# Token mixers of the second block: value products issued two blocks behind the scores, recurrence and convolution issued in pieces

## Chip, cores and metric

The kernel is one program on one core of a Trainium2 chip. The metric is the device time of one execution in microseconds. "Before" and "after" are the kernel without and with the change.

## What is computed

The reference is two transformer-like blocks over 1024 tokens of width 1024, all in float32. The change touches only the token mixers of the second block. With `xn` the normalised input, they are:

```python
proj = xn @ w_in[l]
u, g_lru, q, k, v, z = jnp.split(proj, splits, axis=-1)
uc = centred_depthwise_conv(u, conv_w[l], conv_b[l])
h_fwd = rg_lru(uc, lru_lambda[l, 0], ..., False)
h_bwd = rg_lru(uc, lru_lambda[l, 1], ..., True)
y_a = (h_fwd + h_bwd) * jax.nn.gelu(g_lru)
y_b = banded_alibi_sink_attention(q, k, v, attn_sink[l])
gates = jax.nn.sigmoid(z + b_gate[l]).reshape(bsz, s, N_BRANCH, D_MODEL)
merged = gates[:, :, 0] * y_a + gates[:, :, 1] * y_b
```

In `rg_lru`, two block-diagonal products of `uc` give r and i by a sigmoid, `log_a = -8 * r * softplus(-lam)`, `a = exp(log_a)`, `beta = sqrt(1 - a*a)`, and h is the scan h[t] = a[t] * h[t-1] + beta * i * uc, forwards or backwards in time. The attention has 16 query heads and 4 key/value heads; each block of 128 queries sees its own and the two neighbouring blocks of 128 keys, with a linear distance bias and a sink term in the softmax.

## The kernel before, in words

Every float32 operand is held as two parts, high and low, and a product is three matrix products (high by high, high by low, low by high; `gemm`, L163 to L165), over 128x512 outputs. A weight comes by DMA into `raw`; ScalarE writes its high part (L150) and GpSimd its low part (L151). `split` (L192, L193) does the same for other tensors.

`mixers` runs over j = 0..7; one such stretch is called a period here. Period j does the attention of two heads (`attention(j)`), the three projections of the gates of j (`gates`: g, and two of z), and for j+1 the projection u with its convolution (`lru_front`), the projection q (`att_pair`) and the recurrence's gate products (`lru_gates`). Each projection is two half products of 24 matrix products (`chunk(q)`, 512 tokens each). The recurrence behind the gate products (`lru_rest`) is elementwise: `decay` (ScalarE Exp and Tanh, VectorE L1482), `rate` (ScalarE Square, VectorE L1489 and L1490), `root` (ScalarE Sqrt, L1493, which needs another function table), `scan` (VectorE product L1497 and scans L1499 and L1502, GpSimd sum L1500). Its five pieces are issued one behind each half product of `gates` and, for j = 0, ahead of the half products.

The attention is a generator; `tick` advances it by one step, in the middle and at the end of each half product. Its steps alternate. One issues the scores of query block n+1 (`att_scores`, S below: products L1595 and L1596, the reducing VectorE instruction L1597, the softmax) and the value product of block n-1 (`att_values`, V: L1630, evacuated by ScalarE L1633 and VectorE L1635). The other issues the transposes of block n (`att_turned`, T: L1617, and the split into `pt`, L192 and L193). At j = 2, 4 and 6 the keys and values of the next head group are loaded (`att_group`) and split into `kq` and `vhl`. `merged` (L1685) joins the two branches.

PSUM has eight banks: `mm` three (projections), `ax` two (recurrence gates), `sc` two (scores and transposes), `po` one (value products). The `slot` pool has ten [128 x 1024] buffers, `kq` six, `pt` two. Each engine runs its instructions in one fixed order, which follows the order of issue; an instruction waits for its operands and for the release of its buffer.

## Time and profile before

| | before |
|---|---|
| device time, median of 3 | 3420.71 us (3416.87 to 3430.2) |
| profiled execution: time, span | 3423.95 us, span 3422.2 us |
| mean granted TensorE clock | 0.981 of full |
| TensorE (PE) busy | 3260.1 us, 95% of the span |
| VectorE (DVE), GpSimd (POOL), ScalarE (ACT) busy | 2126.6, 1539.2, 1363.1 us |

The mixers of the second block take the stretch from 1947 to 2650 us. Times below are from the start of the span. Idle time of an engine counts only where the engine that sets the end waits for it. The granted clock has two levels, 2.4 GHz (1.00) and 1.2 GHz (0.50).

### The profile page before, as it was taken

The page shows a single profiled execution, that of the slowest core. Times are in us where ns is not written, and L with a number is a line of the kernel's source. Part 1 is how long each engine was busy: PE and PEld are TensorE (multiplying, and loading weights), DVE is VectorE, ACT ScalarE, POOL GpSimd, SP SyncE. Part 2 cuts the span into 40 slices and gives each one's busy share as a digit, 9 for nine tenths or more (in the row PEclk, how much of TensorE's full clock was granted, in tenths as well). Part 3 has the DMA queues.
Part 4 walks back from the last instruction along what each step waited for, and adds up shares of the span by engine and source line. Part 5 has one row for each costly group of instructions (what it writes and reads, how often), then busy time and mean ns, then how long its engine had stood idle before and what let it go on. Part 6 is the DMA issues. An engine that isn't in the chain of part 4 may idle for free. (4 is left out here: it accounts for less than half of the span.)

```text
span 3422.2 us, 43238 instructions
## 1 busy us (share of the span) xinstructions
PE 3260.1 (95%) x15868; PEld 2695.3 (79%) x15868; DVE 2126.6 (62%) x3438; ACT 1363.1 (40%) x2396; POOL 1539.2 (45%) x991
## 2 busy tenths in 40 slices
PE   7999999999999999999989989999999999999998
PEld 4778888888888878888767867777777778888767
DVE  7554234333667386565798487777776585554786
ACT  4552122211122442222434486666665333233433
POOL 3222233221312775454655433444444775554764
PEclk9999999999999999999999999999999999999999
DMA  6121121244236522221342411111114422222342
GB/s 257 62 105 59 50 68 65 75 157 133 77 119 218 171 89 84 74 96 60 122 164 84 131 33 55 45 54 45 55 48 139 161 99 98 81 81 94 98 132 79
DMA packets 153012, 335.11 MB, mean 98 GB/s; under 512 B 20864, under 2 KB 29184, under 8 KB 152800
## 3 DMA queue, kind: packets, MB, share of 16 engines
q1 hardware_dynamic: 140640, 311.36, 27.5%
q10 hardware_dynamic: 12160, 20.98, 1.7%
q8 instruction: 126, 2.06, 0.3%
q14 instruction: 86, 0.70, 0.1%
HBM read 263.07 MB, written 69.21 MB: 97 GB/s over the span
## 5 line engine op out<-in xcount | busy, mean ns | idle before, releaser
L151 POOL TENSOR_TENSOR wl<-raw,wh 128x1024 fp32r<-128x1024 f32 (+1 forms) x188 | 426.1, 2271 | 742.7 <-ACT wh L150 666.1
L163 PE MATMUL mm<-hl,wh 128*128 128x512 f32 (+1 forms) x1584 | 636.8, 402 | 1.6 <-ACT t L1547 1.4
L165 PE MATMUL mm<-hl,wl 128*128 128x512 f32 (+1 forms) x1584 | 625.4, 395 | 2.8 <-POOL wl L151 2.8
L164 PE MATMUL mm<-hl,wh 128*128 128x512 f32 (+1 forms) x1584 | 624.2, 394 | 0.0
L193 POOL TENSOR_TENSOR wl<-half,wh 128x512 fp32r<-128x512 f32 x308 | 432.1, 1426 | 345.6 <-ACT wh L192 340.3
L150 ACT CAST wh<-raw 128x1024 fp32r<-128x1024 f32 (+3 forms) x189 | 177.3, 940 | 491.6 <-PE mm L164 215.7
L165 PEld LDWEIGHTS mm<-hl,wl 128*128 128x128 f32 (+1 forms) x1584 | 300.9, 190 | 68.0 <-POOL wl L151 3.6
L163 PEld LDWEIGHTS mm<-hl,wh 128*128 128x128 f32 (+1 forms) x1584 | 301.6, 190 | 59.5 <-ACT t L1547 1.8
L164 PEld LDWEIGHTS mm<-hl,wh 128*128 128x128 f32 (+1 forms) x1584 | 301.3, 190 | 58.1 <-issue 0.5
L192 ACT CAST wh<-half 128x512 fp32r<-128x512 f32 x308 | 178.5, 619 | 390.4 <-PE ax L1052 197.2
L1030 DVE TENSOR_TENSOR half<-half 128x512 f32<-128x512 f32 x176 | 204.4, 1200 | 3.0
L1606 POOL TENSOR_SCALAR p<-p,ast 128x384 f32<-128x384 f32 (+1 forms) x64 | 84.1, 1314 | 263.5 <-DVE ast L1604 172.5
L175 PE MATMUL mm<-wh,hl 128*128 128x256 f32 x576 | 166.1, 289 | 3.4 <-ACT wh L150 3.4
L177 PE MATMUL mm<-wl,hl 128*128 128x256 f32 x576 | 164.5, 286 | 1.9 <-POOL wl L151 1.9
L176 PE MATMUL mm<-wh,hl 128*128 128x256 f32 x576 | 164.5, 286 | 0.8 <-DVE hl L193 0.6
L1052 PE MATMUL mm<-hl,wh 128*128 128x512 f32 x360 | 140.6, 391 | 3.3 <-POOL hl L193 3.3
L1051 PE MATMUL mm<-hl,wh 128*128 128x512 f32 x360 | 140.3, 390 | 0.7 <-ACT hl L192 0.7
L1053 PE MATMUL mm<-hl,wl 128*128 128x512 f32 x360 | 140.3, 390 | 0.0
L1051 PE MATMUL ax<-hl,wh 128*128 128x512 f32 x344 | 134.2, 390 | 2.0 <-ACT hl L192 1.3
L1053 PE MATMUL ax<-hl,wl 128*128 128x512 f32 x344 | 134.1, 390 | 0.1
L1052 PE MATMUL ax<-hl,wh 128*128 128x512 f32 x344 | 133.9, 389 | 0.0
L193 POOL TENSOR_TENSOR wl<-raw,wh 128x384 fp32r<-128x384 f32 x96 | 113.1, 1198 | 39.4 <-ACT wh L192 38.8
(419 smaller groups left out, 7996.7 us busy)
## 6 DMA issues: line engine op xcount, KB each, us to landing
half<-in_w_fi SPq DMA_DIRECT2D x196, 256.0 KB, 4.8
hid<-t SPq DMA_DIRECT2D x78, 256.0 KB, 2.0
half<-hid SPq DMA_DIRECT2D x72, 256.0 KB, 4.5
raw<-in_w_ada SPq DMA_DIRECT2D x32, 512.0 KB, 3.8
raw<-in_w_o SPq DMA_DIRECT2D x32, 512.0 KB, 3.9
raw<-in_w_fo SPq DMA_DIRECT2D x32, 384.0 KB, 3.3
slot<-in_w_ada SPq DMA_DIRECT2D x16, 512.0 KB, 10.2
raw<-in_w_u SPq DMA_DIRECT2D x16, 512.0 KB, 3.7
```

What stands on the lines that cost most here:

```text
L150: nc.scalar.copy(hi, r)
L151: self.last_split = (eng or nc.gpsimd).tensor_tensor(lo, r, hi.bitcast(F32), op=ALU.subtract).ins
L163: mm(o, wh[:, k], h[k][q][:, s], start=k == 0, stop=False)
L164: mm(o, wh[:, k], l[k][q][:, s], start=False, stop=False)
L165: mm(o, wl[:, k], h[k][q][:, s], start=False, stop=k == kt - 1)
L175: mm(o, h[k][q][:, s], wh[:, k % 4], start=k == 0, stop=False)
L192: self.nc.scalar.copy(hi, x)
L193: (eng or self.nc.vector).tensor_tensor(lo, x, hi.bitcast(F32), op=ALU.subtract)
L1030: V.tensor_tensor(s, a, b, op=op)
L1051: mm(o, wh[:, k], h, start=k == 0, stop=False)
L1052: mm(o, wh[:, k], l, start=False, stop=False)
L1053: mm(o, wl[:, k], h, start=False, stop=k == 3)
```

## The change

`att_values` for block n is issued two steps of the generator later, together with the scores of block n+2 instead of n+1; `pt` has three buffers instead of two. The transposes take the `ax` banks and no longer share `sc` with the scores; the recurrence's gate products take the `mm` banks of the projections instead of `ax`. The recurrence is cut into eleven pieces and the convolution into three; a new `beat` advances the attention by one step and then issues one piece, and it stands where `tick` stood, in the middle and at the end of each half product. What is left of the pieces is issued ahead of the first gates of j = 0 and ahead of the end of each period. A scratch area for DMA descriptors is made smaller, which gives room for the third `pt`.

```diff
-        self.bg, self.lag, self.loads = deque(), deque(), 0
+        self.bg, self.lag, self.bits, self.loads = deque(), deque(), deque(), 0
...
+    def beat(self):
+
+        self.tick()
+        if self.bits:
+            self.bits.popleft()()
...
             uc = F["uc"] = self.slot()
             cw = lambda k: self.vec("conv_w_2", 8 * k + j)
-            V.tensor_scalar(uc, u, cw(2), self.vec("conv_b_2", j), op0=ALU.mult, op1=ALU.add)
-            for k, (o, i) in ((0, (slice(2, T), slice(0, T - 2))), (1, (slice(1, T), slice(0, T - 1))), (3, (slice(0, T - 1), slice(1, T)))):
+
+            def tap(k, o, i):
                 V.scalar_tensor_tensor(uc[:, o], u[:, i], cw(k), uc[:, o], op0=ALU.mult, op1=ALU.add)
...
+            self.bits.extendleft((parted, sides, centre))
+        return self.proj(self.I["w2_u"][j], evac, self.beat)
...
-                    ps = self.ax_bank()
+                    ps = self.mm_bank()
                     self.gemm(ps, w, *F["c"], q, kt=1)
...
-        return [lambda: decay(0), lambda: (rate(0), decay(1)), lambda: rate(1), lambda: (root(0), root(1)),
-                lambda: (scan(0), scan(1))]
+        bit = lambda f, *a: lambda: f(*a)
+        return [bit(decay, 0), bit(rate, 0, 0), bit(rate, 0, 1), bit(decay, 1), bit(rate, 1, 0), bit(rate, 1, 1), roots,
+                bit(scaled, 0), bit(scan, 0), bit(scaled, 1), bit(scan, 1)]
...
-        tt = self.pp.tile([P, 2, 2, 3 * P], F32R, name="pt")
+        tt = self.pp.tile([P, 2, 2, 3 * P], F32R, name="pt", bufs=3)
         for e in QS:
-            pt = self.pc.tile([P, HQ], F32, name="sc")[:, :nb * P]
+            pt = self.ax_bank()[:, :nb * P]
...
-        p, X = self.att_scores(j, 0, K, Q), None
+        p, X = self.att_scores(j, 0, K, Q), deque()
         yield
         for n in range(8):
             nxt = self.att_scores(j, n + 1, K, Q) if n < 7 else None
-            if n:
-                self.att_values(n - 1, K, X, F["o"])
-            yield
-            X = self.att_turned(n, p)
+            if n > 1:
+                self.att_values(n - 2, K, X.popleft(), F["o"])
+            yield
+            X.append(self.att_turned(n, p))
             p = nxt
             yield
-        self.att_values(7, K, X, F["o"])
+        for n in (6, 7):
+            self.att_values(n, K, X.popleft(), F["o"])
+            yield
...
-            self.step(front(0))
-            rest = self.lru_rest(0, F[0])
+            for c in front(0):
+                c()
+                self.beat()
+            self.bits.extend(self.lru_rest(0, F[0]))
...
                 for c in chunks:
-                    if rest:
-                        rest.pop(0)()
                     c()
-                    self.tick()
+                    self.beat()
+                if not j:
+                    while self.bits:
+                        self.bits.popleft()()
                 for i, c in enumerate(gates):
+                    if i == 1:
+                        self.bits.extend(nxt)
                     c()
-                    self.tick()
-                    if nxt:
-                        nxt.pop(0)()
+                    self.beat()
+                while self.bits:
+                    self.bits.popleft()()
                 self.drain()
                 self.merged(j, F[j])
...
-    nc = bacc.Bacc("TRN2", target_bir_lowering=False, num_devices=1)
+    nc = bacc.Bacc("TRN2", target_bir_lowering=False, num_devices=1, dynamic_dma_scratch_size=8192)
```

The arithmetic is the same; the engines have the same instructions but for two function-table loads of ScalarE fewer. What moves is their order.

First place, TensorE near the end of the period j = 3: the last scores (block 7) and what stands behind them. `sc` are score banks, `pt` the split transposes, `po` the value bank. Before, where `pt_18432` was written by the transposes of block 5, twelve products ahead of these rows:

```order
L1595 MATMUL sc_18462<-kq_17187,kq_17398 128x256
L1596 MATMUL sc_18462<-kq_17188,kq_17398 128x256
L1595 MATMUL sc_18466<-kq_17187,kq_17399 128x256
L1596 MATMUL sc_18466<-kq_17188,kq_17399 128x256
L1630 MATMUL po_18479<-pt_18432,vhl_17201 128x256 x6
L163 MATMUL mm_18508<-hl_14843,wh_18504 128x512
```

After, where `pt_18349` was written by the transposes of block 4, a block earlier:

```order
L1615 MATMUL sc_18451<-kq_17187,kq_17385 128x256
L1616 MATMUL sc_18451<-kq_17188,kq_17385 128x256
L1615 MATMUL sc_18455<-kq_17187,kq_17386 128x256
L1616 MATMUL sc_18455<-kq_17188,kq_17386 128x256
L1650 MATMUL po_18468<-pt_18349,vhl_17201 128x256 x6
L163 MATMUL mm_18489<-hl_14843,wh_18485 128x512
```

The value product now uses transposes that are one block older; the scores stand where they stood.

Second place, TensorE in the middle of the same period, at the second direction of the recurrence's gate products (`slot` operands). Before:

```order
L1595 MATMUL sc_18313<-kq_17187,kq_17398 128x384
L163 MATMUL ax_18296<-slot_18062,wh_18250 128x512
L164 MATMUL ax_18296<-slot_18063,wh_18250 128x512
L165 MATMUL ax_18296<-slot_18062,wl_18251 128x512
L163 MATMUL ax_18301<-slot_18062,wh_18250 128x512
L164 MATMUL ax_18301<-slot_18063,wh_18250 128x512
L165 MATMUL ax_18301<-slot_18062,wl_18251 128x512
L1596 MATMUL sc_18313<-kq_17188,kq_17398 128x384
L163 MATMUL ax_18306<-slot_18062,wh_18250 128x512
L164 MATMUL ax_18306<-slot_18063,wh_18250 128x512
L165 MATMUL ax_18306<-slot_18062,wl_18251 128x512
L1595 MATMUL sc_18317<-kq_17187,kq_17399 128x384
```

After:

```order
L1615 MATMUL sc_18306<-kq_17187,kq_17386 128x384
L163 MATMUL mm_18280<-slot_18161,wh_18239 128x512
L164 MATMUL mm_18280<-slot_18162,wh_18239 128x512
L165 MATMUL mm_18280<-slot_18161,wl_18240 128x512
L163 MATMUL mm_18285<-slot_18161,wh_18239 128x512
L164 MATMUL mm_18285<-slot_18162,wh_18239 128x512
L165 MATMUL mm_18285<-slot_18161,wl_18240 128x512
L163 MATMUL mm_18290<-slot_18161,wh_18239 128x512
L164 MATMUL mm_18290<-slot_18162,wh_18239 128x512
L165 MATMUL mm_18290<-slot_18161,wl_18240 128x512
L1616 MATMUL sc_18306<-kq_17188,kq_17386 128x384
L1650 MATMUL po_18319<-pt_18178,vhl_17201 128x256
```

The gate products now write `mm` banks, three products to a bank, and one half of the scores and the value product stand behind them.

Third place, VectorE at the end of the same period and the load of the next keys (`kq`, `vhl`). Before:

```order
L1490 SCALAR_TENSOR_TENSOR slot_18289<-slot_18289,t512_18565 128x512
L193 TENSOR_TENSOR pt_18582<-sc_18583,pt_18582 128x256
L193 TENSOR_TENSOR pt_18582<-sc_18588,pt_18582 128x256
L1497 TENSOR_TENSOR slot_18289<-slot_18289,slot_18290 128x1024
L1499 SCALAR_TENSOR_TENSOR slot_18290<-slot_18498,slot_18289 128x1024
L1671 SCALAR_TENSOR_TENSOR slot_18457<-t512_18605,slot_18457 128x512
L1635 TENSOR_TENSOR slot_17967<-po_18609,ot_18614 64x128 x2
L193 TENSOR_TENSOR kq_18689<-t512_18690,kq_18688 128x512
L1685 SCALAR_TENSOR_TENSOR slot_17967<-slot_18651,slot_17967 128x512
L193 TENSOR_TENSOR kq_18689<-t512_18695,kq_18688 128x512
L193 TENSOR_TENSOR vhl_18702<-t512_18700,vhl_18702 128x8x64
L1685 SCALAR_TENSOR_TENSOR slot_17967<-slot_18651,slot_17967 128x512
```

After (L1505 and L1506 are the `rate` of before, L1513 the product and L1518 the scan, L1655 the evacuation of `po`, L1708 `merged`, L1617 the reduction of the scores):

```order
L1693 SCALAR_TENSOR_TENSOR slot_18446<-t512_18590,slot_18446 128x512
L1655 TENSOR_TENSOR slot_17967<-po_18594,ot_18601 64x128 x2
L1505 SCALAR_TENSOR_TENSOR t512_18605<-slot_18278,t512_18605 128x512
L1506 SCALAR_TENSOR_TENSOR slot_18278<-slot_18278,t512_18605 128x512
L1513 TENSOR_TENSOR slot_18278<-slot_18278,slot_18279 128x1024
L1655 TENSOR_TENSOR slot_17967<-po_18628,ot_18633 64x128 x2
L1518 SCALAR_TENSOR_TENSOR slot_18279<-slot_18546,slot_18278 128x1024
L1708 SCALAR_TENSOR_TENSOR slot_17967<-slot_18651,slot_17967 128x512
L193 TENSOR_TENSOR kq_18689<-t512_18690,kq_18688 128x512
L193 TENSOR_TENSOR kq_18689<-t512_18695,kq_18688 128x512
L193 TENSOR_TENSOR vhl_18702<-t512_18700,vhl_18702 128x8x64
```

The `rate` instructions of the last half now stand behind the evacuation of the last value product but one, and one `merged` stands ahead of the first split of the keys.

## Rows read from the trace of the kernel before

**Rows 1.** Busy time by stretch (length; PE, PEld, DVE, ACT, POOL; clock): mixers; j=0, 2, 7.

```profile
1947.00:2650.00 703.00, 654.32 (x3136) 534.00 (x3135) 528.79 (x1069) 472.67 (x897) 294.56 (x163) 0.97 0.18 58
1965.00:2051.00 86.00, 73.68 (x351) 59.23 (x351) 71.36 (x138) 70.88 (x123) 32.16 (x17) 0.96 0.11 33
2129.85:2214.73 84.88, 79.31 (x385) 64.96 (x384) 67.76 (x134) 57.81 (x111) 36.35 (x21) 0.98 0.17 55
...
2555.76:2650.00 94.24, 89.28 (x425) 73.16 (x426) 61.79 (x138) 53.58 (x108) 43.83 (x25) 0.96 0.38 127
```

**Rows 2.** TensorE's waits in the mixers: us in total, times, longest.

```profile
PE po L1630 <- DVE pt L193: 20.1, 7, 5.3
PE sc L1595 <- DVE pt L193: 11.8, 13, 1.9
PE po L1630 <- DVE slot L1635: 8.9, 8, 1.2
PE po L1630 <- ACT pt L192: 4.6, 8, 0.7
PE ax L163 <- ACT slot L1467: 1.7, 2, 0.9
```

**Rows 3.** One half-clock stretch of the mixers, and the sum over all eight.

```profile
2300.60:2307.40 6.80, 5.26 (x14) 4.30 (x15) 4.97 (x6) 5.72 (x7) 0.27 (x1) 0.50 0.73 193
...
sum 40.60, PE 31.76 PEld 25.43 DVE 32.14 ACT 30.94 POOL 5.90; mean PE 3.97 PEld 3.18 DVE 4.02 ACT 3.87 POOL 0.74
```

**Rows 4.** Timeline of TensorE at the end of j=3 (start, us; idle before).

```profile
2297.46 0.39 PE L164 MATMUL mm<-hl,wh 128*128 128x512 f32 x1
2297.68 0.39 PE L165 MATMUL mm<-hl,wl 128*128 128x512 f32 x1
2299.31 0.36 PE L1630 MATMUL po<-pt,vhl 128*128 128x256 f32 x1 [1.24 <-DVE slot L1635]
2302.14 1.01 PE L1630 MATMUL po<-pt,vhl 128*128 128x256 f32 x3 [2.47 <-DVE pt L193]
```

**Rows 5.** Timeline of VectorE at the end of period j=3.

```profile
2292.85 0.69 DVE L1671 SCALAR_TENSOR_TENSOR slot<-t,slot 128x512 f32<-128x512 f32 x1
...
2295.77 2.89 DVE L1490 SCALAR_TENSOR_TENSOR slot<-slot,t 128x512 f32<-128x512 f32 x1
2298.59 0.57 DVE L1635 TENSOR_TENSOR slot<-po,ot 64x128 f32<-64x128 f32 x2
...
2301.34 0.74 DVE L193 TENSOR_TENSOR pt<-sc,pt 128x256 fp32r<-128x256 f32 x2
```

**Rows 6.** Timeline of GpSimd there.

```profile
2295.26 5.61 POOL L151 TENSOR_TENSOR wl<-raw,wh 128x1024 fp32r<-128x1024 f32 x2
```

**Rows 7.** Timeline of TensorE in period j=3: second half of a score product.

```profile
2251.87 0.44 PE L1595 MATMUL sc<-kq 128*128 128x384 f32 x1 [1.10 <-DVE pt L193]
```

**Rows 8.** ScalarE by line in the mixers: evacuation of the recurrence's gates.

```profile
L1467 ACT ACTIVATE slot<-ax,lk 128x512 f32<-128x512 f32 x64 | 42.4, 692 | 8.6 <-PE ax L165 6.8 <-DVE slot L1502 1.1 <-DVE ast L1604 0.4
```

**Rows 9.** Timeline of VectorE where keys and values are loaded (end of j=1).

```profile
2134.07 1.23 DVE L1497 TENSOR_TENSOR slot<-slot 128x1024 f32<-128x1024 f32 x1 [1.80 <-ACT slot L1493]
2135.33 2.29 DVE L1499 TENSOR_TENSOR_SCAN slot<-slot 128x1024 f32<-128x1024 f32 x1
...
2138.73 2.28 DVE L193 TENSOR_TENSOR kq<-t,kq 128x512 fp32r<-128x512 f32 x1
2140.93 1.78 DVE L1685 SCALAR_TENSOR_TENSOR slot<-slot 128x512 f32<-128x512 f32 x1
2142.63 1.77 DVE L193 TENSOR_TENSOR kq<-t,kq 128x512 fp32r<-128x512 f32 x1
```

**Rows 10.** Timeline of ScalarE at the end of period j=3.

```profile
2301.49 1.28 ACT L1493 ACT_TABLE_LOAD   x1 [4.68 <-DVE slot L1490]
2302.79 1.06 ACT L1493 ACTIVATE slot<-slot 128x1024 f32<-128x1024 f32 x1
```

**Rows 11.** Busy time in the middle of period j=0.

```profile
1980.00:2015.00 35.00, 29.81 (x140) 23.32 (x139) 34.46 (x57) 26.16 (x47) 17.46 (x8) 0.95 0.09 30
```

More of the change, by code (lines that the diff above doesn't have):

```diff
@@ L1443, in evac, with centre, sides, parted @@
             cw = lambda k: self.vec("conv_w_2", 8 * k + j)
-            V.tensor_scalar(uc, u, cw(2), self.vec("conv_b_2", j), op0=ALU.mult, op1=ALU.add)
-            for k, (o, i) in ((0, (slice(2, T), slice(0, T - 2))), (1, (slice(1, T), slice(0, T - 1))), (3, (slice(0, T - 1), slice(1, T)))):
+            def tap(k, o, i):
                 V.scalar_tensor_tensor(uc[:, o], u[:, i], cw(k), uc[:, o], op0=ALU.mult, op1=ALU.add)
-            ch, cl = self.slot(dt=F32R), self.slot(dt=F32R)
-            self.split(ch, cl, uc, eng=nc.gpsimd)
-            F["c"] = [[[t[:, hs(q)] for q in QS]] for t in (ch, cl)]
-        return self.proj(self.I["w2_u"][j], evac, self.tick)
+            def centre():
+                V.tensor_scalar(uc, u, cw(2), self.vec("conv_b_2", j), op0=ALU.mult, op1=ALU.add)
+                tap(0, slice(2, T), slice(0, T - 2))
+            def sides():
+                tap(1, slice(1, T), slice(0, T - 1))
+                tap(3, slice(0, T - 1), slice(1, T))
+            def parted():
+                ch, cl = self.slot(dt=F32R), self.slot(dt=F32R)
+                self.split(ch, cl, uc, eng=nc.gpsimd)
+                F["c"] = [[[t[:, hs(q)] for q in QS]] for t in (ch, cl)]
+            self.bits.extendleft((parted, sides, centre))
+        return self.proj(self.I["w2_u"][j], evac, self.beat)
     def lru_gates(self, j, F):
@@ L1482, in decay, with rate, roots, scaled @@
             V.scalar_tensor_tensor(F["i", d], F["i", d], 1.0, F["uc"], op0=ALU.add, op1=ALU.mult)
-        def rate(d):
-            for q in QS:
-                b, tr = self.t512(), F["t", d][:, hs(q)]
-                nc.scalar.activation(b, F["a", d][:, hs(q)], AF.Square)
-                V.scalar_tensor_tensor(b, tr, 0.0, b, op0=ALU.max, op1=ALU.mult)
-                V.scalar_tensor_tensor(tr, tr, 0.0, b, op0=ALU.max, op1=ALU.add)
-        def root(d):
-            nc.scalar.activation(F["t", d], F["t", d], AF.Sqrt, scale=0.25)
+        def rate(d, q):
+            b, tr = self.t512(), F["t", d][:, hs(q)]
+            nc.scalar.activation(b, F["a", d][:, hs(q)], AF.Square)
+            V.scalar_tensor_tensor(b, tr, 0.0, b, op0=ALU.max, op1=ALU.mult)
+            V.scalar_tensor_tensor(tr, tr, 0.0, b, op0=ALU.max, op1=ALU.add)
+        def roots():
+            for d in QS:
+                nc.scalar.activation(F["t", d], F["t", d], AF.Sqrt, scale=0.25)
+        def scaled(d):
+            V.tensor_tensor(F["t", d], F["t", d], F["i", d], op=ALU.mult)
         def scan(d):
             a, b, o = F["a", d], F["t", d], F["i", d]
-            V.tensor_tensor(b, b, o, op=ALU.mult)
             if d:
@@ L1577, in evac @@
                 nc.vector.scalar_tensor_tensor(t[b], ps[a], 0.125, t[a].bitcast(F32), op0=ALU.mult, op1=ALU.subtract)
-        return self.proj(self.I["w2_q"][j], evac, self.tick)
+        return self.proj(self.I["w2_q"][j], evac, self.beat)
     def att_scores(self, j, n, K, Q):
@@ L1677, in zb_evac @@
             nc.scalar.activation(F["z"][:, hs(q)], ps, AF.Tanh, bias=self.hbz[:, 8 + j:9 + j], scale=0.5)
-        return self.proj(I["w2_g"][j], g_evac, self.tick) + self.proj(I["w2_z"][j], za_evac, self.tick) + self.proj(I["w2_z"][8 + j], zb_evac, self.tick)
+        return (self.proj(I["w2_g"][j], g_evac, self.beat) + self.proj(I["w2_z"][j], za_evac, self.beat)
+                + self.proj(I["w2_z"][8 + j], zb_evac, self.beat))
     def merged(self, j, F):
```

## Prediction, made before the changed kernel ran

> **What bounds the kernel now.** I read the busy time by stretch first. TensorE is busy for 654.3 of the 703.0 us of the mixers, so it sets their pace; VectorE has 528.8 and ScalarE 472.7 [rows 1]. TensorE has the same products after the change. The mixers can therefore gain only what TensorE loses there, and that is three things.
>
> First its idle time: 703.0 - 654.3 = 48.7 us. Of that, 86.0 - 73.7 = 12.3 lie in the period j=0, 94.2 - 89.3 = 5.0 in j=7, and 31.4 in what is left, which is nearly all j=1 to 6; j=2 has 84.9 - 79.3 = 5.6 [rows 1].
>
> Second its clock. In eight stretches that follow the longer waits, the granted clock is at its lower level, 1.2 GHz; one of them shows 0.50 over 6.80 us, with 5.26 us busy. In all, TensorE is busy for 31.8 us at that level [rows 3]. At 2.4 GHz that work takes half, so 15.9 us are lost: about 2.0 per stretch, by count 4.0 for the two in j=0 and 11.9 for the six at the ends of j=1 to 6.
>
> Third, each wait empties TensorE's pipeline. A product lasts 0.39 us but the next starts 0.22 behind it [rows 4], so a wait costs 0.17 more than its idle time. With 38 waits [rows 2] that is 6.5 us. The three make 71 us, the ceiling of any gain.
>
> Next, the waits by what they wait for, which say what the change can reach. Value products wait for `pt`, 20.1 us behind VectorE and 4.6 behind ScalarE; scores wait 11.8 us for the split of `pt`, since the transposes hold their banks; and value products wait 8.9 us for the evacuation of the one `po` bank [rows 2]. The end of j=3 shows how they arise. The last value product starts at 2299.31 after 1.24 us of idling for the evacuation L1635, and then idles 2.47 for the split of `pt` [rows 4]. VectorE meanwhile ran an L1490 of 2.89 us ahead of L1635 at 2298.59, and the two splits at 2301.34 took 0.74 together [rows 5]. VectorE's work of the recurrence stands ahead of what TensorE needs.
>
> **The change part by part.** I go by the profiled execution, 3424.0 us, which stands 3.2 above the median of 3420.7.
>
> *Value products two blocks back.* V then reads a `pt` one block older. Between the two, a block gives 24 projection products at 0.22, over 5 us, and the scores. The longest of these waits is 5.3, in j=0, so in j=1 to 6 they should all go. What is late next is the transposes, which wait for the softmax; nothing says that they come earlier, and they had no wait there worth a row.
>
> *Transposes in `ax`, three `pt`.* The scores' second half no longer needs the split (1.10 at 2251.87 [rows 7]). Both score banks are then held only by the reduction. Instructions and durations are the same. I count all these waits in j=1 to 6 as gone.
>
> *One `po` bank.* It stays, so its 8.9 us may stay. The last two value products come closer: 12 projection products apart, 2.7 us. But their evacuation no longer stands behind the last two `rate` pieces (third place in the order). The bounds are 0 and 8.9; I take half, 4, as left outside j=0.
>
> So of the 31.4 us of j=1 to 6, 27 go.
>
> *Gate products in `mm`.* Each of the eight groups of a period is three products, 0.66 us, and its evacuation on ScalarE takes 0.69 [rows 8]. Three banks turn round at that pace, but a projection's product behind a group must wait when ScalarE is busy with something else. The trace has two such waits, 1.7 us in total, for the two `ax` banks [rows 2], 0.85 each. Bounds per period: none, or eight waits of 1.4 (two evacuations each), 11 us. I take one of 0.85, since the groups are spread between scores and transposes in the order: 6 us over seven periods.
>
> *Recurrence and convolution in pieces.* The same instructions in another order, the last pieces later against TensorE. While projections cover them they cost nothing. At the ends of j=1, 3 and 5 the cover ends, because the split of the next keys stands behind them on VectorE. Counted from the last `rate` instruction: table load 1.28 and Sqrt 1.06 [rows 10], product 1.23, evacuation 0.57 [rows 5], scan 2.29, `merged` 1.78, first split of the keys 2.28 [rows 9] = 10.5 us. The first scores come 48 products behind the last value product, 48 x 0.22 = 10.6. With the last `rate` about 1 us behind that value product, which I read from the order, the first scores are 0.9 late. Ahead of their reduction stand another 1.77 for the keys, `vhl`, which I take at the same, and 1.78 for `merged`, 5.3 us in all [rows 9], while the next scores come some 3 us later: another 2.4. So 3.3 us per load, bounds 0 (last `rate` well ahead) and 6 (the last two `rate` at 2.89). Three make 10 us. Behind such a wait the clock falls, as it did at these ends before; I keep 2.6 for each (half of the 5.26 [rows 3]), so of 11.9 us of lost clock 4 come back.
>
> Here the Trainium skill has a figure. By the trace the Sqrt starts 1.30 us behind the start of its table load [rows 10]: the load is all that a switch costs. The page "ScalarE: Activation LUTs", section "What ACT_TABLE_LOAD costs", gives about 2.66 us for a switch, with a drain of 1.38 behind the load. The trace does not show that drain. By the page each of the three chains would be 1.4 longer and the gain 4 us smaller; I go by the row.
>
> *Refilling.* Some 25 waits go and some 12 come: 13 x 0.17 = 2 us gained.
>
> *Period j=0.* VectorE is busy for 34.5 of 35.0 us in its middle [rows 11], and the pieces take no work from it. It has 12.3 idle and 4.0 of clock to give; the longest value wait, 5.3 [rows 2], is reachable, and behind it one fall of the clock: I take 7, bounds 0 and 14.
>
> *Period j=7.* There are no projections of a next period. Value products that come later end up behind each other with no product between, so the chain of softmax, transposes and split is bare. I put 6 us of waiting and 2.6 of clock against 5.0 of idling now [rows 1]: a loss of 4, bounds 0 and 8. The start of the mixers, where pieces are issued sooner, gets a loss of 1.
>
> Sum: 27 + 4 + 2 - 10 - 6 + 7 - 4 - 1 = 19 us; to the nearest that I trust, 20. From 3424.0 this is 3404, and on the footing of the median 3401.
>
> **Rivals.**
>
> *Everything is covered.* The keys' split is in time, the gate banks never block, and with the waits the low clock goes too. For it: VectorE has 17 us free in a period of 85 (67.8 busy in j=2 [rows 1]). Against it: j=0, where VectorE is full. Of the ceiling of 71, some 8 stay in j=0 and 3 in j=7: a gain of 60, 3361.
>
> *The waits only move.* The key load takes 6 instead of 3.3 (8 us more) and the whole `po` wait stays (4 more): 7 us are left, 3414. For it: VectorE's instructions at the ends of periods are the same and stay in line.
>
> *VectorE is held up by GpSimd.* An L1490 took 2.89 us beside GpSimd's two L151 (5.61 us from 2295.26 [rows 6]), while L1671, with the same shape and two operands in SBUF, took 0.69 ahead of them; the splits of `pt`, one operand in PSUM, were not drawn out [rows 5]. Spread over the period, more of the recurrence can fall beside GpSimd. If eight more instructions in each period lose 2.2, VectorE has 67.8 + 17.6 = 85.4 us; busy for 34.5 of 35.0, as it is in j=0 [rows 11], it needs 86.7, 1.8 more than the 84.9 of now [rows 1]. Six periods then lose 11 us, what I have for j=0, j=7 and the start gives 2, and the time is 3421 + 9 = 3430. The Trainium skill has this as a rule against the change: in "SBUF — State Buffer", "Who interferes with whom", a VectorE instruction with two SBUF inputs contends with a GpSimd instruction that reads SBUF, and the later one is blocked. The trace agrees, with 2.89 against 0.69.
>
> *Slower: the gate products block the projections.* If every group of gates makes a product wait for two evacuations, 8 x 1.4 = 11 us per period, seven periods lose 78 instead of 6, and the time is 3401 + 72 = 3473. It decides from 6 + (20 + 17) = 43 us, 6 us per period: above that the kernel is slower by over 0.5%. For it: ScalarE has the casts of weights in the same line, and the banks were separate before. Against it: only two waits on this evacuation in the whole trace.
>
> **How the numbers follow.** A measurement of this kernel can tell about 0.5%, 17 us. The forecast has a chance of 0.47, everything covered 0.17, waits that only move 0.18, VectorE held up 0.08, gate products that block 0.10. Faster by over 0.5% (under 3403.6) takes the first rival, four fifths of 0.47 less a share for the forecast's nearness to that line (I put 0.34) and a little of the second: 0.17 + 0.34 + 0.03 = 0.54. Slower takes the last one and a little of the third: 0.10. The rest, 0.36, is no change that can be told. The range reaches from three quarters of the way to everything covered, 3370, to VectorE held up, 3430; outside it lie the last rival and about half of the first, some 2 in 10.
>
> **What would show it.** In the changed profile, the waits of value products for `pt` and of scores for the split should be nearly gone from j=1 to 6; the half-clock stretches should stand only at the key loads, in j=0 and in j=7; the ends of j=1, 3 and 5 should have 2 to 5 us of idling scores, those of j=2, 4 and 6 about 1 on `po`. The periods should be 78 to 80 us without a key load and 82 to 85 with one, and j=7 longer than before. I am wrong if the projections wait for the gates' evacuation more than once a period, if VectorE's recurrence instructions are drawn out beyond 2 us all over the period, or if the wait at the key load is not there.

## The result, and the profile after

The changed kernel takes 3397.65 us (median of 4 runs, 3394.93 to 3398.73). The ratio of the means to the kernel before is 0.9926, with an interval from 0.9914 to 0.9938: 25 us faster (23 by the medians). A fourth run of the kernel before, at 3623.2 us, is a slow one and is left out here as it is in the table above. The forecast was 3401 with a range from 3370 to 3430. The size came out close, but the parts of it did not: its terms for the gate products and for the keys' load were off by 9 and 7 us, in opposite directions, it gave the clock too little, and the experiments show that the edit I gave most of the credit to does nothing alone.

Below, "mixers" is the time between the starts of the same two TensorE products, the 9485th and the 12619th of 15868, in each kernel's profiled execution. Before, that is 702.8 us (1947.2 to 2650.0); after, 674.3. The mixers account for 28.5 us; the span went from 3422.2 to 3395.5, so the rest of the program, which the change does not touch, took 1.8 more in that execution.

Busy time by stretch, changed kernel: mixers, the periods j=2 and j=3, and j=7, each from the last value product of a period to that of the next (columns as in [rows 1]):

```profile
1950.33:2624.64 674.31, 637.38 (x3135) 529.87 (x3134) 514.97 (x1069) 468.50 (x895) 288.29 (x165) 0.99 0.20 63
2130.61:2211.92 81.31, 77.13 (x387) 64.11 (x385) 65.18 (x134) 57.56 (x111) 35.11 (x21) 1.00 0.18 57
2211.92:2291.70 79.78, 76.66 (x386) 64.24 (x385) 59.91 (x131) 56.02 (x108) 34.62 (x21) 1.00 0.15 49
2535.61:2624.64 89.03, 83.93 (x413) 70.74 (x412) 62.50 (x136) 52.13 (x106) 41.29 (x25) 0.98 0.43 142
```

Period j=2 takes 81.3 us where it took 84.9 [rows 1], and VectorE is busy for 65.2 where it was 67.8, with the same instructions. TensorE's idle time in the mixers is 36.9 us (48.7 before), and its busy time fell by 17 us, some 12 of them by the clock (below); where the other 5 come from no view here shows.

What TensorE waits for in the mixers, changed kernel:

```profile
PE mm L163 <- ACT slot L1484: 10.1, 6, 1.7
PE po L1650 <- DVE slot L1655: 9.4, 11, 3.7
PE mm L163 <- DVE kq L1597: 4.7, 6, 0.8
PE po L1650 <- ACT pt L192: 3.6, 7, 0.7
PE sc L1615 <- DVE ast L1617: 3.4, 3, 1.3
PE ax L1637 <- DVE ast L1618: 2.7, 1, 2.7
```

Against [rows 2]: value products no longer wait for VectorE's split of `pt` (20.1 us before), nor scores for it (11.8). New are 10.1 + 4.7 us of gate products that wait for an `mm` bank (all twelve of these waits stand before a gate product, none before a projection), and 3.4 for the reduction of the scores.

TensorE's clock, changed kernel: its three stretches at the lower level, and one stretch at the upper level of which more is said at the end:

```profile
2016.60:2023.40 6.80, 5.69 (x17) 4.75 (x18) 5.02 (x13) 4.89 (x11) 2.71 (x2) 0.50 0.20 59
2091.70:2095.10 3.40, 3.13 (x8) 2.77 (x9) 1.59 (x7) 3.03 (x8) 1.37 (x1) 0.50 0.40 147
2593.50:2596.90 3.40, 3.04 (x13) 2.67 (x14) 2.51 (x10) 2.15 (x7) 2.16 (x2) 0.50 0.32 98
2254.50:2257.90 3.40, 3.40 (x16) 2.88 (x17) 2.72 (x7) 3.37 (x8) 1.37 (x1) 1.00 0.32 117
```

TensorE is busy for 5.69 + 3.13 + 3.04 = 11.9 us at 1.2 GHz. For the kernel before, the sum of 31.8 in [rows 3] does not hold: its windows leave out a stretch in j=0 and cover another one, at the end of j=0, with two windows that reach beyond it. These two stretches, in the kernel before:

```profile
1989.90:1993.30 3.40, 3.40 (x14) 3.11 (x13) 3.31 (x8) 2.48 (x4) 1.75 (x1) 0.51 0.00 0
2048.00:2054.80 6.80, 6.10 (x16) 4.94 (x17) 5.56 (x7) 4.51 (x5) 2.72 (x2) 0.50 0.33 102
```

With them TensorE was busy for 35.0 us in eight stretches, so 17.5 us were lost before and 5.9 are now. None of the three lies behind the end of a period j=1 to 6.

The end of a period, changed kernel, TensorE's last two value products of j=2:

```profile
2208.11 0.88 PE L1650 MATMUL po<-pt,vhl 128*128 128x256 f32 x6
...
2211.57 0.64 PE L1650 MATMUL po<-pt,vhl 128*128 128x256 f32 x4
```

There is no wait in front of either; before, the last one had 1.24 and 2.47 us [rows 4]. VectorE at the same time:

```profile
2204.68 0.80 DVE L1505 SCALAR_TENSOR_TENSOR t<-slot,t 128x512 f32<-128x512 f32 x1
2205.51 0.69 DVE L1506 SCALAR_TENSOR_TENSOR slot<-slot,t 128x512 f32<-128x512 f32 x1
2206.12 0.75 DVE L193 TENSOR_TENSOR pt<-ax,pt 128x256 fp32r<-128x256 f32 x2
...
2210.55 0.57 DVE L1655 TENSOR_TENSOR slot<-po,ot 64x128 f32<-64x128 f32 x2
2211.15 1.39 DVE L1505 SCALAR_TENSOR_TENSOR t<-slot,t 128x512 f32<-128x512 f32 x1
```

The split of `pt` at 2206.12 comes behind one L1505 and one L1506 of 0.80 and 0.69 us; the other pair comes at 2211.15, behind the evacuation L1655. Before, two L1489 and two L1490 stood ahead of that split. Rows 5 shows one of them, the L1490 of 2.89 us; the others, in the kernel before:

```profile
2293.46 2.39 DVE L1489 SCALAR_TENSOR_TENSOR t<-slot,t 128x512 f32<-128x512 f32 x2
...
2299.19 2.22 DVE L1490 SCALAR_TENSOR_TENSOR slot<-slot,t 128x512 f32<-128x512 f32 x1
```

Together they took 2.39 + 2.89 + 2.22 = 7.5 us, while the same instruction takes 0.69 when no GpSimd instruction runs beside it. So 2.8 of these 7.5 us are the block's own, and some 4.7 come from the drawing out beside GpSimd's instructions: the two L151 of [rows 6] and an L1672 just ahead of them.

### The profile page after: what moved, and what is told of

Same layout as the page of the kernel before. It is cut to its first block, busy times and chain, and to the rows that moved or that the text cites. A ratio compares the mean times of both kernels' runs of the same rounds, so it can differ in the third digit from the quotient of the medians.

```text
span 3395.5 us, 43273 instructions
## 1 busy us (share of the span) xinstructions
PE 3242.6 (95%) x15868; PEld 2691.8 (79%) x15868; DVE 2113.0 (62%) x3438; ACT 1359.8 (40%) x2394; POOL 1530.8 (45%) x991
## 5 line engine op out<-in xcount | busy, mean ns | idle before, releaser
L151 POOL TENSOR_TENSOR wl<-raw,wh 128x1024 fp32r<-128x1024 f32 (+1 forms) x188 | 422.3, 2248 | 733.9 <-ACT wh L150 678.7
```

The source lines that it names most:

```text
L151: self.last_split = (eng or nc.gpsimd).tensor_tensor(lo, r, hi.bitcast(F32), op=ALU.subtract).ins
```

## The experiments

All are compared with the kernel before, on the same chip as they. The change has three separable parts: the lag (value product two blocks back, third `pt`), the banks (transposes in `ax`, gate products in `mm`) and the pieces (recurrence and convolution, with `beat`). The first six runs are, with the kernel before and the changed one, all their combinations. The ratio is over several executions; the three columns to its right are of one profiled execution each. Executions of one kernel differ by several us (before: 3416.87 to 3430.2), so a difference of a few us between two mixers is read only beside the ratios.

| kernel | ratio to before, interval | mixers, us | idle before products, us | stretches at half clock, us |
|---|---|---|---|---|
| before | | 702.8 | 48.7 | 41.0 |
| lag | 1.0000, 0.9991 to 1.0010 | 700.7 | 51.6 | 41.0 |
| banks | 0.9993, 0.9984 to 1.0003 | 696.8 | 49.7 | 27.3 |
| pieces | 0.9935, 0.9919 to 0.9952 | 679.6 | 33.2 | 17.1 |
| lag and banks | 0.9986, 0.9977 to 0.9995 | 697.6 | 51.8 | 47.8 |
| lag and pieces | 1.0039, 1.0024 to 1.0053 | 710.4 | 54.1 | 44.4 |
| banks and pieces | 0.9955, 0.9940 to 0.9970 | 683.4 | 38.9 | 17.1 |
| all three (changed) | 0.9926, 0.9914 to 0.9938 | 674.3 | 36.9 | 13.7 |
| lag, po emptied by ScalarE | 1.0014, 1.0005 to 1.0023 | 706.7 | 50.9 | 54.6 |
| changed, po emptied by ScalarE | 1.0026, 1.0015 to 1.0037 | 712.3 | 54.6 | 58.0 |
| recurrence in pieces | 0.9924, 0.9908 to 0.9940 | 675.1 | 33.0 | 13.7 |
| convolution in pieces | 0.9998, 0.9989 to 1.0008 | 703.3 | 47.8 | 41.0 |
| one cut in the recurrence | 0.9952, 0.9937 to 0.9967 | 682.0 | 39.8 | 6.8 |
| changed, gates in both pools | 0.9935, 0.9917 to 0.9954 | 680.2 | 42.4 | 13.7 |

**The lag alone.** The edit, against the kernel before:

```diff
-        tt = self.pp.tile([P, 2, 2, 3 * P], F32R, name="pt")
+        tt = self.pp.tile([P, 2, 2, 3 * P], F32R, name="pt", bufs=3)
...
-            if n:
-                self.att_values(n - 1, K, X, F["o"])
+            if n > 1:
+                self.att_values(n - 2, K, X.popleft(), F["o"])
```

> Only the value product two blocks back and the third pt buffer; banks and pieces as before. Theory 1 (the distance between transposes and value product is what counts): the value products' waits for pt, 24.7 us in the mixers of before, fall below 6, the score waits of 11.8 stay, some of the half-clock stretches go, the mixers become 15 us shorter (688). Theory 2 (the recurrence in one block ahead of the splits on VectorE is what counts, the distance only moves the wait): the value products' waits stay above 15 us and the mixers are within 5 us of 703.

It does nothing: 1.0000. TensorE's first waits in the mixers of this kernel:

```profile
PE po L1636 <- DVE slot L1641: 35.7, 9, 5.2
PE sc L1601 <- DVE pt L193: 13.6, 20, 1.8
```

Theory 1 is half right and its conclusion wrong. The waits for `pt` are gone, as it said, but those for the evacuation of `po` grew from 8.9 us [rows 2] to 35.7, 4.7 at the end of each period from j=1 to 6. Theory 2 said that the wait would move, and it did: the value products still wait, for another result of VectorE.

**The banks alone.** The edit:

```diff
-            pt = self.pc.tile([P, HQ], F32, name="sc")[:, :nb * P]
+            pt = self.ax_bank()[:, :nb * P]
...
-                    ps = self.ax_bank()
+                    ps = self.mm_bank()
```

> Only the banks: transposes in ax, gate products in mm; value product one block back and recurrence in blocks as before. Theory 1: the score waits of 11.8 us go, the gate products' waits of some 15 us (2.45 per period, as in the changed kernel) come, the value products' waits stay: the mixers at 700 to 710 us. Theory 2: the same, since neither holds that the banks matter alone.

Mixers at 696.8, 3 us better than expected; the whole, 0.9993, can't be told from none. The score waits for the split went, as expected. The value products' waits stayed for `pt` (15.2 + 6.3 us) and grew for `po`, from 8.9 to 18.9. The gate products' waits were only 3.6, not 15; why they are shorter here I leave open.

**The pieces alone.** The changed kernel with lag and banks undone:

```diff
-            if n > 1:
-                self.att_values(n - 2, K, X.popleft(), F["o"])
+            if n:
+                self.att_values(n - 1, K, X, F["o"])
...
-            pt = self.ax_bank()[:, :nb * P]
+            pt = self.pc.tile([P, HQ], F32, name="sc")[:, :nb * P]
...
-                    ps = self.mm_bank()
+                    ps = self.ax_bank()
```

> Only the recurrence in eleven and the convolution in three pieces. Theory 1: the value products still have one block, so their waits for pt and the evacuation fall by half at most; the mixers shorter by 5 to 10 us (693 to 698). Theory 2: the waits behind VectorE go, mixers shorter by 20 us or more (under 683).

679.6 us, 23.2 less than before: Theory 2's number, 683 or less. The value products' wait for VectorE's `pt` and for `po` is gone without any lag; the scores' wait for the split stays, at 12.3 us. What came instead are four waits of the scores for their reduction, 11.5 us: 3.0 behind the end of j=0 and 2.8 at each of the three loads of keys, each with a fall of the clock.

**Lag and banks**, the changed kernel without the pieces (recurrence, convolution and `mixers` as before, with the edits of the first two runs).

> The changed kernel with the recurrence and the convolution in blocks and places of before. Theory 1: value and score waits for pt are gone, what is left are the evacuation of po behind the blocks of VectorE (8.9 us of before) and the gate products' 15; mixers at 680 to 688. Theory 2: within 5 us of before, 698 or more.

697.6 us, 5.2 below before and so just outside Theory 2's 5 us, but on its side: waits on `po`'s evacuation are 37.6 us. Two edits that remove 24.7 and 11.8 us of waits by name gain 5 together.

**Lag and pieces**, the changed kernel with the banks of before (the second edit undone).

> The changed kernel with the banks of before: transposes share sc with the scores, gate products in ax. Theory 1: the gate products' waits for banks (14.8 us in the changed kernel) go to below 4, the score waits for the split of pt come back, but less than 11.8 us since VectorE has no long blocks; mixers 668 to 680, so the banks gain nothing or lose a little. Rival (the banks are needed: with shared banks the scores wait again and the clock falls): mixers 685 or more.

Neither theory has it right: this kernel is slower than before by 0.4%, on the rival's side and well past it. TensorE's two largest waits, and VectorE at the end of a period of this kernel:

```profile
PE po L1650 <- DVE slot L1655: 24.5, 7, 3.9
PE sc L1615 <- DVE pt L193: 20.5, 17, 3.6
```
```profile
2130.40 2.22 DVE L1506 SCALAR_TENSOR_TENSOR slot<-slot,t 128x512 f32<-128x512 f32 x1
2132.54 2.83 DVE L1693 SCALAR_TENSOR_TENSOR slot<-t,slot 128x512 f32<-128x512 f32 x1
...
2135.89 0.57 DVE L1655 TENSOR_TENSOR slot<-po,ot 64x128 f32<-64x128 f32 x2
```

Scores wait for the split of `pt` again, more than before (20.5), and the last value product waits 3.86 us, until 2136.61, for the evacuation at 2135.89, behind an L1506 of 2.22 and an L1693 of 2.83. Both can take 0.69: L1506 in the rows of the changed kernel above, L1693, which was L1671, in [rows 5]. So 3.7 us of the two are drawn out beside GpSimd, whose two L151 run from 2129.23 for 5.59 us, and part of this loss may come from where GpSimd's work falls; the run does not separate it. By the measured times, beside the pieces the lag pays only with the banks: with transposes in the scores' banks it costs 30.8 us on top of the pieces (679.6 to 710.4), with banks of their own it gains 9.0 (683.4 to 674.3).

**Banks and pieces**, the changed kernel with the first edit undone.

> The changed kernel with the value product one block back. Theory 1: the value products wait for pt again, at least 10 us of the 24.7 of before, half-clock stretches at the ends of periods come back; mixers 685 to 695. Theory 2 (pieces carry it): mixers within 4 us of 674.

683.4 us, between the two. The value products wait for `pt` again, 18.2 + 6.6 us as Theory 1 says, but in small waits (the 31 for VectorE at most 1.6 each), and the clock does not fall at the ends of periods, which it said it would.

**The lag alone, with `po` emptied by ScalarE.** What was left open is whether the single `po` bank holds the lag back, or VectorE. The edit against the lag alone:

```diff
-        t = self.pp.tile([P, 2, P], F32, name="ot", bufs=1)
+        t, s = (self.pp.tile([P, 2, P], F32, name=nm, bufs=1) for nm in ("ot", "os"))
         nc.scalar.copy(t[:64].rearrange("p a b -> p (a b)"), po[64:128])
+        nc.scalar.copy(s[:64].rearrange("p a b -> p (a b)"), po[:64])
...
-            nc.vector.tensor_tensor(o[64 * e:64 * e + 64, n * P:n * P + P], po[:64, e * P:e * P + P], t[:64, e], op=ALU.add)
+            nc.vector.tensor_tensor(o[64 * e:64 * e + 64, n * P:n * P + P], s[:64, e], t[:64, e], op=ALU.add)
```

> The lag alone, with the po bank emptied by ScalarE alone (two copies of 64 rows to SBUF) and VectorE's two additions reading the copies. The theory after six runs: with the lag the value products no longer wait for pt but for the evacuation of the one po bank, which stands behind the recurrence's blocks on VectorE (35.7 us of waits on it in the lag-alone run). Then the bank comes free without VectorE: those waits fall below 8 us, most half-clock stretches at the ends of periods go, and the mixers fall from 700.7 to 670 to 680 us, so that the lag gains over 20 us without any piece. Rival (what is late is VectorE as a whole, and the next thing behind it stops TensorE just as long): the waits move to the scores or the keys' load and the mixers stay above 692.

The rival holds: 706.7 us. The wait moved again, back to the split of `pt`:

```profile
PE po L1636 <- DVE pt L193: 26.3, 6, 4.4
PE sc L1601 <- DVE pt L193: 16.2, 19, 2.2
```

VectorE at the end of j=2 in this kernel, where L1495 is the first instruction of `rate`:

```profile
2211.62 5.54 DVE L1495 SCALAR_TENSOR_TENSOR t<-slot,t 128x512 f32<-128x512 f32 x2
...
2218.28 0.74 DVE L193 TENSOR_TENSOR pt<-sc,pt 128x256 fp32r<-128x256 f32 x2
```

Whichever result of VectorE TensorE needs at the end of a period, in these runs it comes late, because VectorE is in the recurrence's block, here with 5.54 us for two instructions that take some 1.4 alone. The bank alone was not the cause. The edit is not clean, though: VectorE's additions now have both operands in SBUF and take 449 ns in the mean instead of 280.

**The changed kernel with the same evacuation.**

> The changed kernel with the same evacuation by ScalarE. Its waits on po's evacuation are 9.4 us, 5.6 of them in the first period: by the theory they go and the mixers become 5 to 9 us shorter than 674.3. Rival: ScalarE gets a copy more per value product, 0.37 us, in a line in which the gate products' evacuation is already late (14.8 us of waits), so those grow by as much and the mixers stay at 674 or above.

The rival, and more: 712.3 us. The gate waits grew only from 14.8 to 15.9 us, but scores wait 19.8 us for their reduction (longest 4.9). ScalarE's part of this is argued, not shown: the order of the other engines moved as well, and VectorE's additions took 516 ns in the mean instead of 281.

**The recurrence in pieces alone**, the third run with the convolution whole.

> Only the recurrence in eleven pieces, the convolution whole. The theory: the long waits at the ends of periods came from the recurrence's blocks, so this has nearly all of the 23.2 us that the pieces have together: mixers 680 to 686; the convolution's block still costs the score wait of 1.1 us per period. Rival: the convolution's 6 us block is what makes the clock fall or the chain late, and this run has less than half: above 691.

675.1 us and a ratio of 0.9924: all of the change's gain. The profile is that of its fastest run (3390.87 us; median 3398.97), so the ratio is the better figure.

**The convolution in pieces alone**, the third run with the recurrence's five blocks and places of before.

> Only the convolution in three pieces, the recurrence in its five blocks and places of before. The theory: it takes only the score wait of about 1.1 us per period: mixers 693 to 701. Rival: under 691.

703.3 us, nothing, and less than the theory allowed: not even the score waits for the split went, they stayed at 10.9 us.

**One cut.** The kernel before, with the second direction's `rate` in two pieces:

```diff
-        def rate(d):
+        def rate(d, qs=QS):
-            for q in QS:
+            for q in qs:
...
-        return [lambda: decay(0), lambda: (rate(0), decay(1)), lambda: rate(1), lambda: (root(0), root(1)),
+        return [lambda: decay(0), lambda: (rate(0), decay(1)), lambda: rate(1, [0]), lambda: rate(1, [1]), lambda: (root(0), root(1)),
                 lambda: (scan(0), scan(1))]
```

> The kernel before with one cut: the rate of the second direction is issued as two pieces, one for each half of the tokens, behind two successive half products, so that the table switch, the product and the scans come one half product later; still whole blocks elsewhere, no lag, no bank changed. On VectorE one half of that rate then stands behind the split of the last transposes and the evacuation of the last value products. Theory now: this place alone makes the waits at the ends of periods; the value products' waits for pt fall from 20.1 to below 8 us, half-clock stretches at those ends go, and mixers become 676 to 686 us, most of what the eleven pieces gain. Rival: the gain of the eleven pieces comes from all of the period (rates, decays and scans spread), and the one cut leaves the mixers at 692 or more.

682.0 us, 0.9952: 20.8 of the 28.5 us, for an edit of one line. TensorE's waits for `pt`, and VectorE at the end of j=2 in this kernel:

```profile
PE po L1630 <- ACT pt L192: 4.5, 8, 0.7
PE po L1630 <- DVE pt L193: 2.7, 1, 2.7
```
```profile
2206.09 0.68 DVE L1489 SCALAR_TENSOR_TENSOR t<-slot,t 128x512 f32<-128x512 f32 x1
2206.81 1.67 DVE L1490 SCALAR_TENSOR_TENSOR slot<-slot,t 128x512 f32<-128x512 f32 x1
2208.40 0.57 DVE L1635 TENSOR_TENSOR slot<-po,ot 64x128 f32<-64x128 f32 x2
2209.00 0.76 DVE L193 TENSOR_TENSOR pt<-sc,pt 128x256 fp32r<-128x256 f32 x2
...
2216.38 1.39 DVE L1489 SCALAR_TENSOR_TENSOR t<-slot,t 128x512 f32<-128x512 f32 x1
```

The value products' wait for VectorE's `pt` fell from 20.1 [rows 2] to 2.7 us, the one in j=0. Ahead of the split at 2209.00 stand one L1489 and one L1490, not two of each, and the second pair comes at 2216.38. Only two stretches at half clock are left (2048 and 2478). Part of the wait moved on: at each of the three loads of keys, scores now wait 1.7 to 1.9 us for the split of `kq` and 2.1 for the reduction, 11.8 us in all. And the edit does two things at once, since the square roots, the products and the scans also come one half product later.

**The changed kernel with the gates in both pools:**

```diff
-                    ps = self.mm_bank()
+                    ps = self.ax_bank() if q else self.mm_bank()
```

> The changed kernel with the recurrence's gate products for the first 512 tokens in mm and for the second in ax, with the transposes. The changed kernel loses 14.8 us in seven gate stretches to banks of mm that ScalarE or VectorE has not emptied. Theory: with five banks in turn these fall below 5 us, and the mixers go from 674 to 662 to 668, faster than both kernels. Rival: the transposes, which share ax, now wait for ScalarE's evacuation instead; mixers at 672 or more.

The rival: 680.2 us, 0.9935, no better than the changed kernel. The waits for ScalarE's evacuation went (10.1 us), but those for the q projection's bank grew from 4.7 to 9.2 us and value products wait 8.3 us for ScalarE's half of the split (3.6 before this edit). No run is clearly faster than the changed kernel; the recurrence's pieces alone equal it.

## Why the prediction came out right, and where it was not

**Value products two blocks back: the number right, the reason wrong.** That the time came out close is in part luck: terms that were wrong in opposite directions made up for each other. The prediction had these waits as a matter of distance, and took the transposes as what is late next. The lag alone leaves 0 of it: what is late next is the evacuation of `po`, and with that freed, the split again. In the rows the prediction read this itself ("VectorE's work of the recurrence stands ahead of what TensorE needs") and then priced the pieces at no gain ("While projections cover them they cost nothing"). That is the step that failed. One cut in the recurrence's order on VectorE takes these waits away with no lag.

What stays open is GpSimd's share, a rival that no run tests. Wherever TensorE waits at the ends of periods, the drawing out of the VectorE instructions ahead, beyond the 0.69 us that each takes alone, is of the size of the wait: 4.7 us against 2.47 + 1.24 before, 4.9 against 4.7 in the lag alone, 2.7 against 4.0 with lag and banks, 3.7 against 3.9 with lag and pieces, 4.1 against 4.4 with `po` emptied by ScalarE. The one cut shows that the order of VectorE's line is enough to remove the waits; whether moving GpSimd's weight splits and leaving the block whole would do it too is not shown.

**Transposes in `ax`.** The scores' waits for the split went, as predicted, wherever the banks were changed. With the gate products in `mm`, from which no run separates them, they are alone worth at most 6 us in the mixers and nothing that the ratio can tell (0.9993); their part is that beside the pieces the lag gained only with the banks.

**One `po` bank.** I left 4 us outside j=0; there are 9.4 - 5.6 = 3.8.

**Gate products in `mm`: mis-sized.** 6 us predicted, 14.8 measured: two waits in each of six periods, 1.67 and 0.78, not one of 0.85. TensorE and ScalarE in j=3 of the changed kernel:

```profile
2248.86 0.40 PE L163 MATMUL mm<-slot,wh 128*128 128x512 f32 x1
...
2252.20 0.50 PE L163 MATMUL mm<-slot,wh 128*128 128x512 f32 x1 [1.67 <-ACT slot L1484]
...
2254.49 0.47 PE L163 MATMUL mm<-slot,wh 128*128 128x512 f32 x1 [0.78 <-DVE kq L1597]
```
```profile
2248.76 0.86 ACT L192 CAST pt<-ax 128x384 fp32r<-128x384 f32 x2
2249.51 1.06 ACT L150 CAST wh<-raw 128x1024 fp32r<-128x1024 f32 x1
2250.46 0.59 ACT L1596 ACTIVATE kq<-mm 64x512 fp32r<-64x512 f32 x1
2251.07 0.37 ACT L1653 COPY ot<-po 64x256 f32<-64x256 f32 x1
2251.47 0.69 ACT L1484 ACTIVATE slot<-mm,lk 128x512 f32<-128x512 f32 x1
```

The group at 2252.20 waits for an evacuation which ScalarE starts at 2251.47, behind the split of `pt`, a weight's cast of 1.06 us, the q projection and a copy. The prediction took one wait at the 0.85 us of the two in [rows 2]; what stands ahead in ScalarE's line made it 1.67, and the bank of the q projection added a second. The banks alone do not make this size: with the same banks these waits are 3.6 us in the banks alone, 5.7 with the lag, and 0.7 with the pieces and no lag. Why all three together bring them to 14.8 is open. By the prediction's own sign, a wait for the gates' evacuation more than once a period, it came out at the limit: one such wait a period, but of a gate product, and a second one for another bank.

**Keys' load: mis-sized the other way.** 3.3 us and a fall of the clock at each of three loads were predicted, 10 + 7.8 us. Measured are 1.05 to 1.29 us, 3.4 in all, and no fall, below the 2 to 5 us that the prediction named as its sign. The chain itself is there: with the pieces alone, on the banks of before, the scores wait 2.8 us at each load and the clock falls behind each. With the banks and the pieces, without the lag, it is 1.2 to 1.6 us and no fall. ScalarE, VectorE and TensorE at the end of j=3 of the changed kernel:

```profile
2290.02 1.28 ACT L1510 ACT_TABLE_LOAD   x1
2293.08 1.06 ACT L1510 ACTIVATE slot<-slot 128x1024 f32<-128x1024 f32 x1 [1.78 <-DVE slot L1506]
```
```profile
2298.72 4.58 DVE L193 TENSOR_TENSOR kq<-t,kq 128x512 fp32r<-128x512 f32 x2
2303.23 2.88 DVE L193 TENSOR_TENSOR vhl<-t,vhl 128x512 fp32r<-128x512 f32 x1
```
```profile
2302.73 0.28 PE L1615 MATMUL sc<-kq 128*128 128x256 f32 x1
...
2307.16 0.44 PE L1615 MATMUL sc<-kq 128*128 128x384 f32 x1 [1.05 <-DVE ast L1617]
```

The table load, which I had in the chain at 1.28 us, was done at 2291.30, while ScalarE waited for VectorE; the Sqrt needed no load behind the last `rate`. The figure of the Trainium skill (page "ScalarE: Activation LUTs", section "What ACT_TABLE_LOAD costs") for a drain behind the load can't be judged there. At the next load of the same trace it can: 1.28 us from 2295.90, and its function starts at 2297.19, so no drain of 1.38 us stands behind it, and the prediction was right to go by its row. The first scores at 2302.73 do not wait; the next wait 1.05 us for the reduction, which stands behind the two splits of the keys (4.58 us) and that of the values (2.88), longer than in [rows 9].

**The clock.** Predicted were 4 us back at the ends of periods; 11.6 came back in all (17.5 less 5.9): behind the ends of j=1 to 6 and behind the loads it does not fall any more. This and the loads made up for the gates.

**By period.** To the last value product of j=0 the changed kernel gained 3.9 us (7 - 1 predicted); over j=1 to 6 27.2 (17 predicted: 27 + 4 + 2 - 10 - 6); in j=7 it lost 2.6 (4 predicted). The sum is 28.5, where 19 was worked out and 20 taken; each is between the starts of the same-numbered products, taken at the changed kernel's last value products. Up to twelve products more stand ahead of these than before, so the split between the periods hangs on the mark: from each kernel's own last value product to its next, j=0 gained 2.9, j=1 to 6 23.5 and j=7 2.2, and no loss in j=7 shows. The term of 2 us for refilling has little behind it: 40 waits became 38, not 13 fewer.

**The rivals.** "VectorE is held up by GpSimd" went the other way. VectorE's two instructions of `rate` in the mixers of the changed kernel:

```profile
L1505 DVE SCALAR_TENSOR_TENSOR t<-slot,t 128x512 f32<-128x512 f32 x32 | 28.4, 889 | 7.5 <-ACT t L1504 6.8
L1506 DVE SCALAR_TENSOR_TENSOR slot<-slot,t 128x512 f32<-128x512 f32 x32 | 24.2, 755 | 0.8
```

L1506 takes 755 ns in the mean where L1490 took 1455 (46.4 us over the same 32), because fewer of them begin beside GpSimd's weight splits: 13 of 32 before, one after. The rule of the Trainium skill ("SBUF — State Buffer", "Who interferes with whom") stands: the trace agrees, with 2.22 and 2.83 against 0.69 in the run with lag and pieces; but pieces spread over the period met GpSimd less often, not more. In the rows the prediction cited for operands in PSUM, the splits of `pt` at 2301.34 [rows 5] come after GpSimd's instructions (2295.26 and 5.61 us [rows 6]) have ended and show nothing of it; the L1635 at 2298.59, 0.57 us for two beside GpSimd, does. "Gate products block the projections" was there in another form, gate products that wait for each other's banks, at 2.45 us per period, under the 6 at which it would have decided. "Everything is covered" did not come: 36.9 us of idling are left in the mixers. "The waits only move" is what the lag alone shows, not the whole change.

## What to carry to other kernels

When the engine that sets the end waits for another, look at what stands ahead of the wanted instruction in that engine's line and whether it is long by itself or drawn out by another engine, before you lengthen the distance between producer and consumer; here a longer distance alone only picked the next late result. Edits can need each other: try every combination, since one of three here, the lag, was worth nothing alone, cost 31 us beside the pieces and gained 9 beside pieces and banks. And a block of work in a line is worth cutting first where a short, urgent instruction stands behind it: one cut had, by the ratios, 0.48% where the recurrence's eleven pieces had 0.76% and all fourteen 0.65%, though the intervals of the one cut and of the fourteen overlap.

## What the runs showed of the hardware

The clock's falls do not follow the length of a wait alone. The waits of 1.67 and 0.78 us at the gates are the same in six periods of the changed kernel. Behind those at 2089.69 and 2091.97 the clock was at 0.50 from 2091.7 on for 3.4 us; behind those at 2252.20 and 2254.49 it stayed at 1.00 (fourth row of the clock's windows above). What else decides it these runs don't show.

VectorE's `rate` instruction was drawn out where it began later than a weight split of GpSimd, and not where it began first. Of the 32 L1490 in the mixers of the kernel before (128x512, both tensors in SBUF), the 13 that began while an L151 of GpSimd ran took 2.2 to 2.9 us and the other 19 took 0.68 to 0.69. In the changed kernel one of the 32 L1506 began so and took 2.77; six began 0.06 to 0.07 us ahead of an L151 and took 0.69.
